# First GLU weights split ahead of the gated rows in halves, one operand's buffers placed lowest, and the last prompt tile's store issued by SP

## The chip, the cores and the metric

One core of a Trainium2 chip runs the whole program; its cores' engines are TensorE (PE, with its weight loads as PEld), VectorE (DVE), ScalarE (ACT), GpSimd (POOL) and SyncE (SP). The metric is the device time of one execution in microseconds, as a median over several runs.

## What is computed

One layer of a hybrid decoder is applied to 512 prompt tokens and to 64 sample tokens (8 sequences of 8), with shared weights. It has an attention branch (three gated branches over compressed, selected and window keys) and a state-space branch; the part of the second that the change touches is the gated linear unit (GLU) behind it, and the merge that follows.

```python
def s5_branch(u, h0_re, h0_im, ssm_par, glu_w, glu_b):
    y, hr, hi = s5_scan(...)
    y = jax.nn.gelu(y.reshape(B, T, D_SSM))
    out = (y @ glu_w[0] + glu_b[0]) * jax.nn.sigmoid(y @ glu_w[1] + glu_b[1])
    return out, hr, hi

def merge_out(x, o_att, z_att, y_ssm, z_ssm, g_merge, w_att_out, w_ssm_out, w_o, ln_g, ln_b):
    p_att = (o_att * jax.nn.silu(z_att)) @ w_att_out
    p_ssm = (y_ssm * jax.nn.silu(z_ssm)) @ w_ssm_out
    g_att, g_ssm = jnp.split(g_merge, 2, axis=-1)
    merged = jax.nn.sigmoid(g_att) * p_att + jax.nn.sigmoid(g_ssm) * p_ssm
    return layer_norm(ALPHA * x + merged @ w_o, ln_g, ln_b)
```

## The kernel before

Every large product is made of three matmuls in a reduced-precision format: each operand is split into a high part, which ACT copies with rounding (L108), and a low part, the difference, which DVE computes (L121, or L124 with a scale). The three matmuls are issued by `mm3` at L129 (high, high), L130 (high, low operand) and L131 (low weights, high). `split` is therefore one ACT instruction and, behind it, one DVE instruction, and the first matmul of a product waits for ACT, the second and third for DVE.

The order of instructions on each engine is not the order of the source. A scheduler with its own timing model places them when the program is built; each engine then works through its list in order, and SP's list is the queue from which most loads are issued.

The work around the change, in order of time:

- The 512 prompt tokens pass attention in four tiles of 128 (`prompt_tile`, i = 0 to 3). Each tile ends by multiplying its accumulator with the gate rows (`ast`, DVE, L1084) and storing the product to the DRAM scratch `aD` (L1085, issued by ACT). `aD` is read again near the end (L1610).
- Then `sample` begins. `attend_setup` loads the selection matrix `selt` (L1217, SP) and multiplies the gates by it (L1220, eight small matmuls on PE). The loads of the state-space rows `y` (L1548, 32 of them) and of the GLU weights `or` (L1511) are held back by `issue_after` until the load of `selt` has been issued.
- The sample attention works on four pairs of sequences (w = 0 to 3). The first three are woven with the compression of cached keys. The last pair is woven with `ssm_out`, which is the GLU and the product with `w_ssm_out`.
- `ssm_out` takes its buffers from a pool that overlies the memory of the compression, which has ended by then: scratch, ring, four pairs of operand buffers `ah`/`al` (`pair(0)` to `pair(3)`), two sets of weight tiles. The order of the first requests sets the order of the addresses.
- It splits the four `y` tiles (128 by 576 elements, written through an access pattern that turns the order of tokens) into `ah`/`al`, one ACT and one DVE instruction each. Then it walks over four column tiles of the GLU weights. `weights` loads 128 by 1024 elements, first half for the linear factor and second half for the sigmoid factor, and splits them in one go. For each half of the tokens (288 each) it makes the sigmoid product first and then the linear one; each product is four `mm3`, so twelve matmuls of 288 columns. One GLU column tile is 48 matmuls.
- `output` forms the attention product, the merge, the product with `w_o` and the layer norm.

Of the kernel before, what the change touches and what calls it, by code (L numbers as in the profile page):

```python
# [85 lines left out]
def rr(ap, pat, **kw):  # L86
    return ap.rearrange(pat, **kw)


class Hybrid:  # L90
# [899 lines left out]
    def prompt_tile(self, i, KT, kczs, vcp, bt):  # L990

        nc, pp = self.nc, self.pp
# [4 lines left out]
        q0 = i * 128  # L997
        n = q0 + 128
# [3 lines left out]
        for br in range(2):  # L1002
            P4s = []
            for g in range(2):
# [3 lines left out]
                for r in range(4):  # L1008
                    p = self.psum("S", [128, 512])
# [37 lines left out]
        p = self.psum("S", [128, 4, 2, 64])  # L1047
# [34 lines left out]
        st = pp.tile([128, 4, 128], F, name="ast", tag="ast", bufs=1)  # L1082
        nc.sync.dma_start(st[:], rr(self.zD[0:4], "r p t -> p r t")[:, :, q0:q0 + 128])
        V.tensor_tensor(st[:], rr(acc[:], "p (r q) -> p r q", r=4), st[:], op=OP.mult)  # L1084
        nc.scalar.dma_start(self.aD[:, :, q0:q0 + 128], st[:])  # L1085


    def gather(self, out, cache, idx):
# [413 lines left out]
        return [p.tile([128, 8, 128], d, name=nm, tag=nm, bufs=2)  # L1502
                for p, nm, d in ((self.py, "or", F), (self.pd, "oh", FR), (self.pd, "ol", FR))]

    def weights(self, pieces):

        w, hi, lo = self.weight_tiles()
        at = 0
        for src, n in pieces:
            with self.tc.issue_after(self.selt_dma.ins):  # L1510
                self.wdma = self.nc.sync.dma_start(w[:, at:at + n, :] if n > 1 else w[:, at, :], src)  # L1511
            at += n
        self.split(hi[:, :at], lo[:, :at], w[:, :at])
        return hi, lo

    def ring(self, d=FR):
# [9 lines left out]
    def ssm_out(self):  # L1526

        nc, A, pd = self.nc, self.A, self.pd
        V, G = nc.vector, nc.gpsimd
        TT, TS, ST = V.tensor_tensor, V.tensor_scalar, V.scalar_tensor_tensor  # L1530
        self.halves = [slice(h * 288, h * 288 + 288) for h in range(2)]

        self.scratch("z")
        self.ring()
        for ct in range(4):
            self.pair(ct)
        self.weight_tiles()
        bg = pd.tile([128, 2, 4], F, name="bg")
        with nc.allow_non_contiguous_dma("bias"):
            nc.sync.dma_start(bg[:], rr(A["ssm_glu_b"], "k (t p) -> p k t", p=128))  # L1540
        TS(bg[:, 1], bg[:, 1], 0.5, None, op0=OP.mult)
        gh, gl = [], []
        for ct in range(4):
            y = self.py.tile([128, TOK], F, name="y", tag="y", bufs=4)
            ys = rr(self.yD[ct * 8:ct * 8 + 8], "g (t c) n -> g c t n", t=8)
            for g in range(8):
                with self.tc.issue_after(self.selt_dma.ins):
                    nc.sync.dma_start(rr(y[g * 16:(g + 1) * 16], "c (t n) -> c t n", t=8), ys[g])  # L1548
            hi, lo = self.pair(ct)
            self.split(rr(hi, "p (n t) -> p t n", t=8), rr(lo, "p (n t) -> p t n", t=8), rr(y[:], "p (t n) -> p t n", t=8))  # L1550
            gh.append(hi)
            gl.append(lo)

        sh, sl = [], []
        gw = rr(A["ssm_glu_w"], "k (t p) c -> p k t c", p=128)
        for ct in range(4):
            c = slice(ct * 128, (ct + 1) * 128)
            hi, lo = self.weights([(gw[:, 0, :, c], 4), (gw[:, 1, :, c], 4)])
            z, th, ln = self.scratch("z"), self.scratch("th"), self.scratch("ln")
            nc.sync.dma_start(z[:], self.zD[4 + ct])  # L1560
            for s in self.halves:
                for k in (1, 0):
                    p = self.bank()
                    for t in range(4):
                        self.mm3(p[:, :288], (hi[:, 4 * k + t], lo[:, 4 * k + t]), (gh[t][:, s], gl[t][:, s]), t == 0, t == 3)
                    if k:
                        self.act(th[:, s], p[:, :288], AF.Tanh, scale=0.25, bias=bg[:, 1, ct:ct + 1])
                    else:
                        self.act(ln[:, s], p[:, :288], AF.Identity, scale=0.5, bias=bg[:, 0, ct:ct + 1])
                    yield  # L1570
            ST(ln[:], th[:], 1.0, ln[:], op0=OP.add, op1=OP.mult)
            G.tensor_tensor(ln[:], ln[:], z[:], op=OP.mult)
            hi, lo, _ = self.ring()
            self.split(hi, lo, ln[:])
            sh.append(hi)
            sl.append(lo)

        ws = rr(A["w_ssm_out"], "(t p) c -> p t c", p=128)
        self.merged = []
        for c2 in range(4):  # L1580
            self.merged += self.ring(F)[0:2]
            hi, lo = self.weights([(ws[:, :, (2 * c2 + u) * 128:(2 * c2 + u + 1) * 128], 4) for u in range(2)])
            for u in range(2):
                ct = 2 * c2 + u
                if ct == 0:
                    self.glu_dma = self.wdma
                tg = self.scratch("tg")
                nc.sync.dma_start(tg[:], self.gD[8 + ct])
                for s in self.halves:
                    p = self.bank()  # L1590
                    for t in range(4):
                        self.mm3(p[:, :288], (hi[:, 4 * u + t], lo[:, 4 * u + t]), (sh[t][:, s], sl[t][:, s]), t == 0, t == 3)
                    ST(self.merged[ct][:, s], tg[:, s], 1.0, p[:, :288], op0=OP.add, op1=OP.mult)
                    yield
# [136 lines left out]
```

## Time and profile before

| what | value |
|---|---|
| median of 3 runs | 892.15 us (891.99 to 892.65) |
| profiled execution | 889.58 us, span from first to last instruction 887.8 us |
| PE busy | 849.6 us (96% of the span), 7276 matmuls |
| DVE busy | 568.8 us (64%) |
| ACT busy | 426.2 us (48%) |
| POOL busy | 196.0 us (22%) |
| mean granted TensorE clock | 0.981 of full |

The profile is taken from one execution by the hardware profiler, and times in it count from the start of its span. A timeline row gives the start, the busy time, the engine, the line, the operation, what it writes and reads and how many instructions were merged; in square brackets stands how long the engine had been idle before it and who released it. In the chain of work a row gives start, length, engine, tile and line of one piece of the chain that ended last. [...]

### The profile page before, as it was taken

Reading aid. Unit: us, or ns where it says so; the run is one execution under the profiler, and the core shown is the slowest. Engines: PE = TensorE matmul, PEld = TensorE weight load, DVE = VectorE, ACT = ScalarE, POOL = GpSimd, SP = SyncE. Lnnn points to the kernel's source line nnn. Section 1 sums busy time; section 2 is a strip of 40 time slices with the busy share of each in tenths; the row PEclk is TensorE's granted clock in tenths of the full one; section 3 lists DMA queues with packets and bytes.
Section 4 is the critical chain, followed back from the end, with each engine's and each line's share of the span. In section 5 each row is a group of like instructions: output and inputs, shape, how many; then the busy total and the mean of one; then the engine's idle time right before and its main releaser. Section 6 shows DMA issues by size and latency. Waiting matters only on the chain.

```text
span 887.8 us, 18479 instructions
## 1 busy us (share of the span) xinstructions
PE 849.6 (96%) x7276; PEld 747.8 (84%) x7276; DVE 568.8 (64%) x1559; ACT 426.2 (48%) x876; POOL 196.0 (22%) x249
## 2 busy tenths in 40 slices
PE   8999999999999988999989999999999979999996
PEld 8999999999999967787757878787878758889885
DVE  3469973855354479988627767766764463448784
ACT  4224462223254365768535656555555565545420
POOL 0322719300042211121211323241321101200000
PEclk9999999999999979999979999999999989999999
DMA  8385526365687352323457746383726164849331
GB/s 279 95 201 165 148 67 193 113 203 150 208 247 239 135 133 96 120 96 120 148 182 216 264 164 261 120 313 116 285 97 238 61 236 145 283 129 277 109 107 48
DMA packets 116039, 151.03 MB, mean 170 GB/s; under 512 B 29352, under 2 KB 93224, under 8 KB 111600
## 3 DMA queue, kind: packets, MB, share of 16 engines
q1 hardware_dynamic: 89072, 65.02, 25.6%
q0 software_dynamic: 17824, 80.16, 25.2%
q10 hardware_dynamic: 9056, 4.67, 1.8%
q8 instruction: 57, 0.93, 0.4%
q14 instruction: 30, 0.25, 0.1%
HBM read 134.02 MB, written 19.93 MB: 173 GB/s over the span
## 4 chain that ended last, share of the span: by engine, by line
PE 65%; DVE 11%; DMA 7%; issue 5%; POOL 4%; ACT 4%; SPq 3%; POOLq 0%; DVEq 0%; ACTq 0%
PE p_mm L130 11%; PE p_mm L129 10%; PE p_mm L131 10%; PE p_tr L135 7%; PE p_S L1237 4%; PE p_ca L129 3%; PE p_ca L131 3%; PE p_ca L130 3%; DVE xt L892 2%; PE p_acc L1246 2%; DMA gc<-in_cache_kv_cmp,idx 2%; PE p_acc L1036 2%; DMA relx<-in_rel_bias 1%; DMA wraw<-in_w_in 1%; DVE evl L121 1%
## 5 line engine op out<-in xcount | busy, mean ns | idle before, releaser
L130 PE MATMUL p_mm<-evl,w1h 128*128 128x256 f32 (+1 forms) x512 | 153.8, 300 | 6.3 <-DVE evl L121 6.2
L129 PE MATMUL p_mm<-evh,w1h 128*128 128x256 f32 (+1 forms) x512 | 151.1, 295 | 1.1 <-ACT w1h L108 0.6
L131 PE MATMUL p_mm<-evh,w1l 128*128 128x256 f32 (+1 forms) x512 | 148.2, 290 | 0.9 <-DVE w1l L121 0.9
L121 DVE TENSOR_TENSOR evl<-xt,evh 128x512 fp32r<-128x512 f32 x128 | 87.0, 684 | 52.1 <-ACT evh L108 51.7
L130 PEld LDWEIGHTS p_mm<-evl,w1h 128*128 128x128 f32 x512 | 98.7, 193 | 24.8 <-DVE evl L121 13.1
L108 ACT ACTIVATE evh<-xt 128x512 fp32r<-128x512 f32 x128 | 80.1, 628 | 79.7 <-PE p_mm L131 75.2
L1091 POOL DMA_INDIRECT gc<-in_cache_kv_cmp,idx x64 | 65.5, 1024 | 206.7 <-DVE xt L892 188.9
L129 PEld LDWEIGHTS p_mm<-evh,w1h 128*128 128x128 f32 x512 | 98.9, 193 | 8.7 <-ACT kt L108 2.4
L131 PEld LDWEIGHTS p_mm<-evh,w1l 128*128 128x128 f32 x512 | 98.6, 193 | 5.8 <-issue 4.1
L892 DVE STREAM_TRANSPOSE xt<-gc 128x256 f32<-128x256 f32 x256 | 90.5, 410 | 5.2 <-DMA gc<-in_cache_kv_cmp,idx 4.6
L131 PE MATMUL p_mm<-xTh,wlo 128*128 128x288 f32 x272 | 81.0, 298 | 0.0
L130 PE MATMUL p_mm<-xTl,whi 128*128 128x288 f32 x272 | 81.0, 298 | 0.0
L129 PE MATMUL p_mm<-xTh,whi 128*128 128x288 f32 x272 | 80.9, 298 | 0.0
L108 ACT ACTIVATE pt<-p_tr 128x512 f32<-128x512 f32 x76 | 43.5, 591 | 29.3 <-PE p_tr L135 29.2
L341 DVE TENSOR_TENSOR wlo<-wraw,whi 128x512 fp32r<-128x512 f32 (+1 forms) x56 | 37.5, 728 | 25.4 <-ACT whi L108 25.4
L1091 POOL DMA_INDIRECT g<-in_cache_kv_slc,idx x32 | 32.6, 1018 | 92.9 <-PE p_acc L1246 65.7
L108 ACT ACTIVATE kt<-p_tr 128x512 f32<-128x512 f32 x72 | 40.7, 594 | 24.2 <-PE p_tr L135 24.2
L130 PEld LDWEIGHTS p_mm<-xTl,whi 128*128 128x128 f32 x272 | 51.3, 189 | 0.2 <-issue 0.2
L129 PEld LDWEIGHTS p_mm<-xTh,whi 128*128 128x128 f32 x272 | 51.3, 189 | 0.2 <-issue 0.2
L108 ACT ACTIVATE whi<-wraw 128x2048 fp32r<-128x2048 f32 (+2 forms) x24 | 37.1, 1563 | 29.9 <-DMA wraw<-in_w_in 9.4
L131 PEld LDWEIGHTS p_mm<-xTh,wlo 128*128 128x128 f32 x272 | 51.4, 189 | 0.0
L135 PE MATMUL p_tr<-cst,P 128*128 128x128 f32 x304 | 47.1, 284 | 0.6 <-ACT P L108 0.5
(527 smaller groups left out, 2105.4 us busy)
## 6 DMA issues: line engine op xcount, KB each, us to landing
wraw<-in_w_in SPq DMA_DIRECT2D x11, 1024.0 KB
wraw<-in_w_in SPq DMA_DIRECT2D x10, 512.0 KB
gD<-zst POOLq DMA_DIRECT2D x16, 288.0 KB, 3.2
tg<-gD SPq DMA_DIRECT2D x16, 288.0 KB
wn<-in_state_win_kv POOLq DMA_DIRECT2D x4, 1024.0 KB, 6.2
wor<-in_w_o SPq DMA_DIRECT2D x8, 512.0 KB
out<-in_state_win_kv SPq DMA_DIRECT2D x8, 504.0 KB
wraw<-in_w_in SPq DMA_DIRECT2D x3, 1056.0 KB
```

The lines of the kernel that those rows point to most:

```text
L108: return self.nc.scalar.activation(out, in_, func, **kw)
L121: eng.tensor_tensor(lo, src, hi.bitcast(F), op=OP.subtract)
L129: mm(out, lhi, rhi, start=start, stop=False, **kw)
L130: mm(out, lhi, rlo, start=False, stop=False, **kw)
L131: mm(out, llo, rhi, start=False, stop=stop, **kw)
L135: return self.nc.tensor.transpose(out, in_, self.ident[:k, :k])
L341: (eng or self.nc.vector).tensor_tensor(lo[:, kl, :n], w[:, kl, :n], hi[:, kl, :n].bitcast(F), op=OP.subtract)
L892: self.nc.vector.transpose(out=out, in_=in_)
L1036: mm = nc.tensor.matmul(acc[gr[g]], self.kvn[:, kt, c0 + g * 64:c0 + (g + 1) * 64], PTs[g][:], start=br == 0 and kt == 0, stop=False, skip ...
L1091: self.nc.gpsimd.indirect_dma_start(out=rr(out, "c s v g d -> c (s v g d)"), out_offset=None, in_=src, in_offset=bass.IndirectOffsetOnAxis ...
L1237: mm = self.nc.tensor.matmul(out[r], self.qb[:, w, r], keys[b], start=True, stop=True)
L1246: self.nc.tensor.matmul(acc[r], PT[:, r], vals(b)[:, g * 64:(g + 1) * 64], start=start, stop=stop, skip_group_check=True)
```

## The change

The store of the last prompt tile (i = 3) is issued by SP; the other three stay with ACT. In `ssm_out` the buffers of the fourth operand pair are requested first and so lie lowest, which moves the other requests up by one pair. The first GLU weights are split before the `y` rows, their second half (sigmoid factor) before their first. The `y` rows are split in halves of 288 tokens, all four operands' first halves ahead of all second halves. The other three GLU weight tiles are split as before. No arithmetic is added or removed.

```diff
@@ prompt_tile
-        nc.scalar.dma_start(self.aD[:, :, q0:q0 + 128], st[:])
+        (nc.sync if i == 3 else nc.scalar).dma_start(self.aD[:, :, q0:q0 + 128], st[:])
@@ weights
-    def weights(self, pieces):
+    def weights(self, pieces, order=(slice(0, 8),)):
...
-        self.split(hi[:, :at], lo[:, :at], w[:, :at])
+        for s in order:
+            self.split(hi[:, s], lo[:, s], w[:, s])
@@ ssm_out
+        self.pair(3)
         self.scratch("z")
         self.ring()
-        for ct in range(4):
+        for ct in range(3):
             self.pair(ct)
...
-            self.split(rr(hi, "p (n t) -> p t n", t=8), rr(lo, "p (n t) -> p t n", t=8), rr(y[:], "p (t n) -> p t n", t=8))
+            ys4.append([rr(v, pat, t=8) for v, pat in ((hi, "p (n t) -> p t n"), (lo, "p (n t) -> p t n"), (y[:], "p (t n) -> p t n"))])
...
+        glu0 = glu_weights(0, order=(slice(4, 8), slice(0, 4)))
+        for n in (slice(0, 36), slice(36, 72)):
+            for ct in range(4):
+                self.split(*[v[:, :, n] for v in ys4[ct]])
...
-            hi, lo = self.weights([(gw[:, 0, :, c], 4), (gw[:, 1, :, c], 4)])
+            hi, lo = glu_weights(ct) if ct else glu0
```

On SP, at the end of the prompt attention (`ast` is the last tile's gated product, `selt` the selection matrix):

```order
 L1083 DMA ast<-zD 128x4x128 x2
+L1085 DMA aD<-ast 512x1x128
 L1217 DMA selt<-cst 64x512
-L1548 DMA y<-yD 16x8x72 x32
+L1555 DMA y<-yD 16x8x72 x32
 L1511 DMA or<-in_ssm_glu_w 128x4x128 x4
```

The store now stands ahead of the load of `selt`, and with it ahead of the 32 `y` loads; from ACT's list, where it stood ahead of the copies `kc` and `kn`, it is gone.

On ACT, where the last pair's window attention hands over to the GLU (`ah` are the operands' high parts, `oh` the weights'):

```order
 L108 ACTIVATE Pn,smw<-Pn,nmw 128x64
-L108 ACTIVATE ah_8725<-y 128x8x72
-L108 ACTIVATE ah_8738<-y 128x8x72
-L108 ACTIVATE ah_8751<-y 128x8x72
-L108 ACTIVATE ah_8764<-y 128x8x72
-L108 ACTIVATE oh<-or 128x1024 x2
+L108 ACTIVATE oh<-or 128x512 x2
+L108 ACTIVATE ah_8725<-y 128x8x36
+L108 ACTIVATE ah_8736<-y 128x8x36
+L108 ACTIVATE ah_8747<-y 128x8x36
+L108 ACTIVATE ah_8758<-y 128x8x36
```

The first operand that a matmul can use is now ready after three instructions instead of five. The second halves follow, then the second weight tile.

On PE, the first GLU products in the changed kernel:

```order
L135 MATMUL p_tr<-cst,Pn 64x128
L129 MATMUL p_mm<-ah_8725,oh 128x288 x2
L130 MATMUL p_mm<-al_8726,oh 128x288
L131 MATMUL p_mm<-ah_8725,ol 128x288
L129 MATMUL p_mm<-ah_8736,oh 128x288
L130 MATMUL p_mm<-al_8726,oh 128x288
L131 MATMUL p_mm<-ah_8725,ol 128x288
L129 MATMUL p_mm<-ah_8736,oh 128x288
```

Two products of the first token half advance together, operand by operand. 34 GLU matmuls and the product `p_S<-pcs` now stand ahead of the window's `p_acc` matmuls; before, it was 27 GLU matmuls, with `p_S<-pcs` behind `p_acc`.

## Rows read from the trace of the kernel before

**Rows 1.** By stretch: us, then busy and (instructions) of PE, PEld, DVE, ACT, POOL.

```profile
455.70:465.80 10.10, 9.72 (x39) 7.76 (x39) 2.73 (x10) 2.42 (x4) 2.13 (x3) 0.50 0.99 354
466.00:705.00 239.00, 233.89 (x2479) 194.69 (x2482) 159.33 (x495) 134.63 (x269) 60.52 (x59) 1.00 0.55 194
717.20:721.90 4.70, 0.04 (x2) 0.02 (x1) 4.12 (x6) 4.70 (x6) 0.00 (x0) 0.63 0.24 101
721.90:725.20 3.30, 3.28 (x12) 2.93 (x13) 3.26 (x5) 2.00 (x5) 0.00 (x0) 0.50 0.10 28
728.90:832.00 103.10, 102.82 (x977) 92.20 (x976) 62.65 (x153) 55.66 (x104) 9.76 (x9) 1.00 0.67 207
```

**Rows 2.** Timeline of PE around the start of the GLU.

```profile
716.95 0.27 PE L135 MATMUL p_tr<-cst,Pn 128*64 128x128 f32 x1
721.88 0.61 PE L129 MATMUL p_mm<-ah,oh 128*128 128x288 f32 x1 [4.66 <-ACT oh L108]
```

**Rows 3.** Timeline of ACT, same place.

```profile
716.65 4.33 ACT L108 ACTIVATE ah<-y 128x576 fp32r<-128x576 f32 x4
720.78 2.00 ACT L108 ACTIVATE oh<-or 128x1024 fp32r<-128x1024 f32 x2
722.68 0.49 ACT L108 ACTIVATE pcs<-pcs,mxc 128x255 f32<-128x255 f32 x1
```

**Rows 4.** Timeline of DVE, same place.

```profile
717.16 0.16 DVE L1451 TENSOR_TENSOR sw<-sw,gr 128x1 f32<-128x1 f32 x1
717.90 3.43 DVE L121 TENSOR_TENSOR al<-y,ah 128x576 fp32r<-128x576 f32 x3 [0.58 <-ACT ah L108]
...
722.44 2.35 DVE L121 TENSOR_TENSOR ol<-or,oh 128x1024 fp32r<-128x1024 f32 x2
724.71 0.16 DVE L1370 RECIPROCAL smc<-smc 128x1 f32<-128x1 f32 x1
```

**Rows 5.** Timeline of ACT: the same kind of copy, 64 elements wide.

```profile
804.89 0.69 ACT L108 ACTIVATE ah<-zs 128x64 fp32r<-128x64 f32 x4 [0.38 <-DVE zs L1606]
805.49 1.05 ACT L108 ACTIVATE woh<-wor 128x1024 fp32r<-128x1024 f32 x1
```

**Rows 6.** Chain of work: GLU matmuls at either clock, and what follows them.

```profile
722.73 0.24 PE p_mm L129
...
726.64 0.13 PE p_mm L130
...
727.43 0.83 PE p_acc L1246 x40
728.26 0.63 PE p_S L1374 x2
```

**Rows 7.** Timeline of PE at the end of the prompt attention.

```profile
452.10 1.07 PE L1078 MATMUL p_acc<-pcT,vcp 32*64 32x512 f32 x4 [0.47 <-ACT pcT L108]
455.03 0.66 PE L1173 MATMUL p_ca<-w,hs 128*128 128x64 f32 x4 [1.86 <-ACT kc L108]
455.62 1.90 PE L1220 MATMUL p_S<-gs,selt 64*128 64x24 f32 x8
```

**Rows 8.** Timeline of ACT, same place.

```profile
453.94 0.52 ACTq L1085 DMA_DIRECT2D aD<-ast  x1
454.50 0.47 ACT L108 ACTIVATE kc<-p_ca,kb 128x255 f32<-128x255 f32 x1 [2.46 <-DVE ml L1401]
```

**Rows 9.** Timeline of SP's DMA issues, 430 to 485 us.

```profile
437.12 0.51 SPq L1217 DMA_DIRECT2D selt<-cst  x1
450.86 30.27 SPq L1548 DMA_DIRECT2D y<-yD  x32
```

**Rows 10.** DMA packets from 454.9 to 456.4 us: queue, packets, MB, share (q10 is ACT's).

```profile
q10 hardware_dynamic: 528, 0.26, 64.3%
q0 software_dynamic: 10, 0.08, 36.2%
```

**Rows 11.** DMA packets from 438.5 to 442.5 us (q1 is SP's).

```profile
q0 software_dynamic: 77, 0.50, 31.3%
q1 hardware_dynamic: 80, 0.13, 15.1%
```

**Rows 12.** Chain of work: matmuls of the compression before and after 466 us.

```profile
465.68 0.21 PE p_mm L131
...
467.35 0.12 PE p_mm L131
```

More of the change, by code (lines that the diff above doesn't have):

```diff
@@ L1541, in ssm_out, with glu_weights @@
         TS(bg[:, 1], bg[:, 1], 0.5, None, op0=OP.mult)
-        gh, gl = [], []
+        gw = rr(A["ssm_glu_w"], "k (t p) c -> p k t c", p=128)
+        def glu_weights(ct, **kw):
+            c = slice(ct * 128, (ct + 1) * 128)
+            return self.weights([(gw[:, 0, :, c], 4), (gw[:, 1, :, c], 4)], **kw)
+        gh, gl, ys4 = [], [], []
         for ct in range(4):
@@ L1549, in ssm_out @@
             hi, lo = self.pair(ct)
-            self.split(rr(hi, "p (n t) -> p t n", t=8), rr(lo, "p (n t) -> p t n", t=8), rr(y[:], "p (t n) -> p t n", t=8))
+            ys4.append([rr(v, pat, t=8) for v, pat in ((hi, "p (n t) -> p t n"), (lo, "p (n t) -> p t n"), (y[:], "p (t n) -> p t n"))])
             gh.append(hi)
             gl.append(lo)
+        glu0 = glu_weights(0, order=(slice(4, 8), slice(0, 4)))
+        for n in (slice(0, 36), slice(36, 72)):
+            for ct in range(4):
+                self.split(*[v[:, :, n] for v in ys4[ct]])
         sh, sl = [], []
-        gw = rr(A["ssm_glu_w"], "k (t p) c -> p k t c", p=128)
         for ct in range(4):
-            c = slice(ct * 128, (ct + 1) * 128)
-            hi, lo = self.weights([(gw[:, 0, :, c], 4), (gw[:, 1, :, c], 4)])
+            hi, lo = glu_weights(ct) if ct else glu0
             z, th, ln = self.scratch("z"), self.scratch("th"), self.scratch("ln")
```

## The prediction

> **What bounds the kernel now.** I read the rows by stretch first. PE is the bound: from 466 to 705 us it is busy 233.89 of 239 us, from 728.9 to 832 us 102.82 of 103.10 [rows 1]. Time is therefore won or lost where PE stands still or runs at half clock, and what PE loses or gains there moves everything behind it. Two such places are touched. From 717.2 to 721.9 PE does nothing, while ACT is busy all of the 4.70 us [rows 1]: the timelines show the last transpose of the window branch at 716.95, then 4.66 us of idle time ended by ACT's `oh` [rows 2], because ACT first makes four `ah` and only then `oh` [rows 3]. After the pause the clock is at 0.50 until about 725.2 [rows 1]. The second place is the end of the prompt attention: PE is idle for 1.86 us before L1173, for `kc` [rows 7], and ACT was held up 2.46 us ahead of `kc` because the store of `aD` stood in front of it, waiting for DVE's `ast` [rows 8]. From 455.7 to 465.8 the clock is again at 0.50 [rows 1].
>
> **Part one, the start of the GLU.** First the prices. On ACT four `ah` of 576 elements take (720.78 - 716.65) / 4 = 1.03 us each, `oh` of 1024 takes (722.68 - 720.78) / 2 = 0.95 [rows 3], and a copy of 64 takes (805.49 - 804.89) / 4 = 0.15 [rows 5]. From 64 and 1024 the cost per instruction is 0.10 us, the rest goes with the elements. So half an `oh` is 0.53 us and half an `ah` 0.57. On DVE `al` is (3.43 us for three) about 1.11 each and `ol` (724.71 - 722.44) / 2 = 1.13 [rows 4]; with the same 0.10 a half is about 0.61.
>
> [...]
>
> New schedule, starting where ACT is free, 716.65 [rows 3]: `oh` halves ready at about 717.2 and 717.8, the first half `ah` at 718.4 to 718.5, the next three 0.57 apart, two of the second halves by 721.2, then `pcs` (0.5 us), the other two by 722.8. DVE is free at 717.3 [rows 4]: `ol` halves to 718.7, first half `al` ready at 719.3, then one per 0.61 with the small operations between, the last second half at 723.9, `pcs` at 724.1. So PE starts at 718.5 instead of 721.88, does two matmuls, and has steady work from 719.35.
>
> How far it gets depends on the clock. A GLU matmul takes 0.24 us at half and 0.13 at full clock [rows 6]. I compare at the end of the window's `p_acc`, when the changed order has done 34 GLU matmuls, `p_S<-pcs` (0.63) and `p_acc` (0.83). The kernel before has done 27 of them, `p_acc` and `p_S` at 728.89 [rows 6]; with the other seven, 7 x 0.13 = 0.9, it would be at 729.8. Three cases:
>
> - The clock falls as before and returns after as much steady work as before, 3.3 us from 721.88 to 725.2, so at 722.65: 2 + 3.3 / 0.24 = 15.75 matmuls by then, 18.25 x 0.13 = 2.4 to 725.0, and 1.46 to 726.5. Gain **3.3 us**.
> - It stays low until 725.2 as in the trace: 2 + 24.5 matmuls by then, 7.5 x 0.13 = 1.0, 1.46, end 727.7. Gain 2.1 us.
> - It never falls, the pause now being 1.3 us and not 4.66: PE then waits for DVE, `pcs` at 724.1, end 725.75. Gain 4.0 us.
>
> I take 3.3; the ends are 2.1 and 4.0.
>
> **Part two, the store on SP.** ACT no longer waits: `kc` can start at 452.1, L1173 right after the `p_acc` that ends at 453.2, and the idle 1.86 us is gone. But the next work on PE, L1220, needs `selt`. Before, SP issued that load at 437.12 [rows 9], long ahead. Now it stands behind the store, which cannot be issued before `ast` is ready, at 453.94 [rows 8]. With one issue of about 0.51 us [rows 9] `selt` is issued at 454.45. Its landing has no row at this place. From below: the store's packets, 0.26 MB issued at 453.94, are through at 456.4 [rows 8, 10], 2.5 us after the issue; `selt` by that lands at 456.95, and L1220 starts 1.3 us later than at 455.62 [rows 7]. From above: `selt` itself, issued at 437.12 beside a POOL gather, had its 0.13 MB moved between 438.5 and 442.5 [rows 9, 11], up to 5.4 us; that gives 459.85, 4.2 us late. I take 1.4, near the lower end, since until 456.4 the gathers have only 10 packets in flight [rows 10]: the DMA engines are nearly free, and `selt` follows the store on SP's queue.
>
> What of the 1.4 us reaches the end: this stretch runs at half clock [rows 1]. If the clock returns at the same moment, the work put off is done at 0.12 instead of 0.21 us per matmul [rows 12], and 1.4 x 0.12 / 0.21 = **0.8 us** is lost; if the return moves along, 1.4. Ends: 0.7 (1.3 late, clock as before) and 4.2. Queued behind the store on SP are also the `y` and `or` loads: they start some 4 us later, took 30.27 us [rows 9], and are not used before 716.65, so they cost nothing.
>
> [...]
>
> **The rest.** The buffers of the fourth operand change no instruction and no duration; they change what the first splits wait for, and in the trace those start the moment ACT is free [rows 3], so I cost this at nothing. The cover is the window's exponentials; without it the price would be the wait of `ah` for its memory, at most the 4.7 us of the pause. Behind 728.9 the scheduler has put attention and GLU matmuls in another order, with the same instructions; PE had 0.28 us of idle time in 103.10 there [rows 1]. I cost it at nothing and give it 0.8 us either way, since PE arrives earlier and the loads for the output stage may not.
>
> **Sum.** -3.3 + 0.8 = -2.5 us. The profiled execution took 889.58 us (span 887.8), which gives 887.1; the median of the runs is 892.15, 2.57 us more than the profiled one, and the forecast stands against that: **889.65 us**. A measurement of this kernel can tell about 0.2%, 1.8 us, from no change.
>
> **The rivals.**
>
> 1. The gain is real but small: the clock stays low until 725.2 (2.1 us) and the return near 465.8 moves with the stall (1.4 us). Sum -0.7: **891.45 us**, no change that can be told. For it: both low stretches follow a pause and lasted 3.3 and 10 us of work [rows 1], and the new start of the GLU has gaps between operands. Against it: 0.5 us and less per gap. Chance 0.31, with neighbouring mixtures.
> 2. Slower: `selt` lands behind the gathers. POOL's transfers start about when the store is through [rows 10]; if `selt` shares the engines with them, it takes what it took before, L1220 is 4.2 us late, and if the clock's return is put off by 3.3 us more than that, (1 - 0.12 / 0.21) of it [rows 12], 1.4, is lost too. With the lower gain of the GLU, 2.1: +3.5, **895.65 us**; it decides against the forecast once the delay on PE at 455.62 passes the gain by 1.8 us. For it: rows 11. Against it: rows 10. Chance 0.11.
> 3. The store costs only its issue: `selt` is there in time, by whatever order the queue takes, and PE keeps 0.52 us of ACT's issue [rows 8]. Then -3.3 - 0.5: **888.35 us**. [...] Rows 7 to 9 leave little room for it. Chance 0.07, on the side of faster.
> 4. The change does not do what it says: a split waits for a load or for memory, and PE starts at 721.9 after all. Then only part two is left, +0.8, **892.95 us**. The `y` and `or` loads are done over 200 us earlier [rows 9]; this is within the 0.31.
>
> **How the numbers follow.** The forecast with its own ends (gain 2.1 to 4.0, loss 0.7 to 1.4, 0.8 for the rest) runs from 888.05 to 892.25 and has 0.51; the two cases of a stronger gain bring faster to 0.58. No change has 0.31, slower 0.11. The range 887.8 to 893.0 takes in the forecast, rivals 1, 3 and 4 and leaves out most of rival 2.
>
> **What would show it.** In the profile of the changed kernel: `aD` on SP's queue near 454 and `selt` half a microsecond behind; `kc` on ACT near 452.1; PE waiting before L1220 until about 457; first GLU matmul some 1.3 us after the last window transpose, not 4.66; `p_acc<-wn` and `p_S<-pcs` together about 2.5 us earlier than at 727.43, counted from 887.8. The prediction is wrong if the first GLU matmul still waits over 3 us, if L1220 starts before 456 or after 458.5, or if PE has more than 1 us of new idle time between 729 and 832.

## The result, and the profile after

The changed kernel takes **899.18 us** (median of 5 runs, 896.46 to 904.72) against 892.15 us before: the ratio is 1.0082, with a 95% interval of 1.0058 to 1.0106. It is slower by 7.0 us, where 2.5 us faster was forecast; the time lies outside the range. Run once more later (e10) it was 898.61 us against 891.98, 1.0064 (1.0036 to 1.0092). The profiled execution took 898.94 us with a span of 897.1 us, 9.3 us more than that of before.

Where the 9.3 us are is found by cutting both spans at the same instructions of PE's timeline. The cuts are the first `p_acc<-pcT` of L1078 in the last prompt tile, the first matmul of L1237 (the product with `kc`), the last window transpose and the first GLU matmul; each figure is a difference of two start times.

```
stretch                                before   changed   difference
start to L1078                         452.10    456.24    +4.14
L1078 to L1237                           5.35     11.33    +5.98
L1237 to the last window transpose     259.50    258.17    -1.33
transpose to the first GLU matmul        4.93      1.50    -3.43
first GLU matmul to the end            165.92    169.86    +3.94
```

**The end of the prompt attention.** PE's timeline of the changed kernel, to be held against [rows 7] (start, us, engine, line, operation, count, and in brackets the idle time with what ended it):

```profile
456.24 1.07 PE L1078 MATMUL p_acc<-pcT,vcp 32*64 32x512 f32 x4 [0.47 <-ACT pcT L108]
457.25 0.66 PE L1173 MATMUL p_ca<-w,hs 128*128 128x64 f32 x4
465.74 1.90 PE L1220 MATMUL p_S<-gs,selt 64*128 64x24 f32 x8 [7.83 <-DMA selt<-cst]
```

L1173 now follows L1078 without a pause: the 1.86 us of [rows 7] are gone, as forecast. L1220 then waits 7.83 us for `selt`. SP's and POOL's timelines say what surrounds that load:

```profile
458.08 0.62 SPq L1085 DMA_DIRECT2D aD<-ast  x1
458.79 0.59 SPq L1217 DMA_DIRECT2D selt<-cst  x1
459.48 6.54 SPq L1555 DMA_DIRECT2D y<-yD  x8
```

```profile
458.09 0.93 POOL L1091 DMA_INDIRECT g<-in_cache_kv_slc,idx  x1 [19.20 <-PE p_ca L1173]
459.33 0.94 POOL L1091 DMA_INDIRECT g<-in_cache_kv_slc,idx  x1 [0.30 <-issue]
460.57 0.94 POOL L1091 DMA_INDIRECT g<-in_cache_kv_slc,idx  x1 [0.30 <-issue]
461.51 0.77 POOL L1331 DMA_DIRECT2D wn<-in_state_win_kv  x1
```

`selt` is issued 0.71 us behind the store (0.51 was forecast), but L1220 starts only 6.95 us after that issue. POOL issues three gathers and a load of 1 MB in the same four microseconds. The DMA view shows the packets of the two queues (q1 is SP's, q0 POOL's), first from 459 to 461 us, then from 461 to 462.6, then from 462.6 to 465.7:

```profile
q1 hardware_dynamic: 528, 0.26, 52.0%
q0 software_dynamic: 12, 0.10, 27.6%
...
q0 software_dynamic: 54, 0.44, 81.9%
q1 hardware_dynamic: 3, 0.01, 1.6%
...
q0 software_dynamic: 118, 0.85, 86.8%
q1 hardware_dynamic: 146, 0.14, 18.4%
```

The 528 packets are the store's. For the next 1.6 us SP's queue moves three packets, `selt`'s first, while POOL's queue holds 81.9% of the DMA engines' time; the rest of `selt` comes through in the third stretch, between POOL's packets. Read packet by packet, its 64 packets of 2 KB run from 462.27 to 464.52 us, 3.5 to 5.7 us after the issue, and L1220 starts 1.2 us behind the last.

**The start of the GLU.** PE's timeline, where [rows 2] had a pause of 4.66 us:

```profile
725.74 0.27 PE L135 MATMUL p_tr<-cst,Pn 128*64 128x128 f32 x1
727.24 0.58 PE L129 MATMUL p_mm<-ah,oh 128*128 128x288 f32 x2 [1.22 <-ACT ah L108]
728.04 0.61 PE L130 MATMUL p_mm<-al,oh 128*128 128x288 f32 x1 [0.23 <-DVE al L121]
```

ACT's and DVE's timelines at that place answer to [rows 3, 4]; a half `ah` is 3.40 / 6 = 0.57 us and a half `ol` 1.29 / 2 = 0.65:

```profile
725.43 1.13 ACT L108 ACTIVATE oh<-or 128x512 fp32r<-128x512 f32 x2
726.47 3.40 ACT L108 ACTIVATE ah<-y 128x288 fp32r<-128x288 f32 x6
```

```profile
726.08 1.29 DVE L121 TENSOR_TENSOR ol<-or,oh 128x512 fp32r<-128x512 f32 x2
727.29 1.92 DVE L121 TENSOR_TENSOR al<-y,ah 128x288 fp32r<-128x288 f32 x3
```

**The clock and the tail.** Three stretches by window (us, then busy time and number of instructions of PE, PEld, DVE, ACT, POOL, granted clock of PE as a share of full speed, busy share of the DMA engines, GB/s), the first two to be read against [rows 1]:

```profile
457.90:475.00 17.10, 8.88 (x37) 7.13 (x37) 2.57 (x15) 2.42 (x4) 3.58 (x4) 0.50 0.91 286
727.60:731.00 3.40, 3.17 (x14) 2.96 (x13) 3.40 (x7) 3.40 (x9) 0.00 (x0) 0.50 0.55 161
810.00:830.00 20.00, 17.45 (x130) 16.96 (x129) 16.40 (x35) 11.64 (x21) 0.00 (x0) 1.00 0.90 266
```

The clock is at half for 17.1 us around the stall instead of 10.1, and for 3.4 us at the GLU instead of some 6.8 (all of 721.9 to 725.2, and the part of the pause that makes its mean 0.63). In the last stretch PE is idle for 2.55 us, where before it was busy nearly all through [rows 1]. PE's waits from the last window transpose to the end:

```profile
PE p_mm L131 <- DVE ol L121: 1.7, 1, 1.7
PE p_mm L129 <- ACT ah L108: 1.2, 1, 1.2
PE p_tr L135 <- DMA g<-in_cache_kv_slc,idx: 0.9, 1, 0.9
PE p_ca L129 <- ACT ah L108: 0.8, 1, 0.8
PE p_mm L130 <- DVE al L121: 0.2, 1, 0.2
```

The 1.2 and 0.2 belong to the start of the GLU. The 1.7 for `ol` and the 0.8 for `ah` lie at 825.69 and 813.63 us, in the output stage, which no instruction of the change touches; the 0.9 is a gather of the last sample attention.

### The profile page after: what moved, and what is told of

Same layout as the page of the kernel before. It is cut to its first block, busy times and chain, and to the rows that moved or that the text cites. A ratio compares the mean times of both kernels' runs of the same rounds, so it can differ in the third digit from the quotient of the medians.

```text
span 897.1 us, 18480 instructions
## 1 busy us (share of the span) xinstructions
PE 849.5 (95%) x7276; PEld 747.4 (83%) x7276; DVE 570.8 (64%) x1564; ACT 426.4 (48%) x881; POOL 194.5 (22%) x249
## 4 chain that ended last, share of the span: by engine, by line
PE 68%; DVE 11%; DMA 8%; issue 4%; POOL 4%; ACT 3%; SPq 1%; DVEq 0%; ACTq 0%; POOLq 0%
PE p_mm L130 11%; PE p_mm L131 10%; PE p_mm L129 10%; PE p_tr L135 8%; PE p_S L1237 4%; PE p_ca L129 3%; PE p_ca L131 3%; PE p_ca L130 2%; PE p_acc L1246 2%; PE p_acc L1036 2%; DMA g<-in_cache_kv_slc,idx 2%; DMA bt<-vD 1%; DMA wraw<-in_w_in 1%; PE p_mm L365 1%; DMA wor<-in_w_o 1%
```

## The experiments

Three causes were open: `selt` (theory A), the tail (B, later T) and the start (C). e1 to e4 and e9 to e11 ran on one chip (number 13 on record), e5 to e8 on a second (4), e12 on a third (9), each time with the kernel before beside them. The chip of the first measurement is not on record. The stretches of each run are those of one profiled execution; two executions of the changed kernel (the first and e10) differ by 1.1 us from the last transpose to the end.

**e1: the GLU part without the store.**

```
-        (nc.sync if i == 3 else nc.scalar).dma_start(self.aD[:, :, q0:q0 + 128], st[:])
+        nc.scalar.dma_start(self.aD[:, :, q0:q0 + 128], st[:])
```

> The changed kernel with the last tile's store back on ACT, the GLU part and the buffers kept. Theory A (the loss is selt, issued behind the store on SP and landing 7 us after its issue): PE waits under 2 us before the selt matmuls, for kc as before, the GLU part gains its 3.3 us, and the run is 2 to 4 us faster than the kernel before. Theory B (the tail: a new order of attention, GLU and output matmuls behind 729 us costs 3 us or more by itself): the wait for selt is gone, but the run is within 1 us of the kernel before, and the profile shows PE idle before ah or ol between 800 and 830 us. Theory C (the start: the first 436 us of the changed kernel are 4 us longer for a reason that belongs to the change): the run is 1 to 2 us slower than before.

Measured: 892.30 us, ratio 1.0002 (0.9979 to 1.0025). PE's timeline has no wait for `selt`, the old wait for `kc`, and the new start of the GLU:

```profile
456.47 1.12 PE L1173 MATMUL p_ca<-w,hs 128*128 128x64 f32 x4 [1.87 <-ACT kc L108]
...
719.44 0.53 PE L129 MATMUL p_mm<-ah,oh 128*128 128x288 f32 x2 [1.22 <-ACT ah L108]
```

The first GLU matmul comes 1.50 us after the last transpose (717.95), so the 3.4 us are there. But from that transpose to the end of the span it takes 171.65 us, where before took 170.85. Theory B's time came true, not A's: the GLU part gains, and the tail takes it all back. The sign that B named did not come: PE does not wait for `ah` or `ol` between 800 and 830 us; its waits behind the start of the GLU are for `ring` (0.9), `tg` (1.0) and the gather (0.7). From the first GLU matmul to the end e1 takes 4.3 us more than before; what is not in these waits was not traced.

**e2: the store on SP alone**, the same line put into the kernel before.

> The kernel before with the last tile's store on SP and nothing else. Theory A: selt is issued about half a us behind the store and lands about 7 us later, PE stands still 6 to 9 us before the selt matmuls and gets back 2 us at kc; 4 to 6 us slower than before. Forecast's own term (selt lands 2.5 to 3 us after its issue): 0.7 to 1.4 us slower. Theory B: within 1 us of before until 729 us.

Measured: 901.57 us, ratio 1.0100 (1.0078 to 1.0122), 9.2 us slower; more than any theory gave. PE's timeline:

```profile
456.88 0.66 PE L1173 MATMUL p_ca<-w,hs 128*128 128x64 f32 x4
464.97 1.90 PE L1220 MATMUL p_S<-gs,selt 64*128 64x24 f32 x8 [7.43 <-DMA selt<-cst]
```

`selt` was issued at 458.42, 6.55 us before L1220, and L1078 to L1237 takes 10.93 us instead of 5.35, +5.6. What A lacked is the other end: from the last window transpose to the end it is 173.48 us, +2.6, with nothing changed in the GLU or behind it. The scheduler has put PE's matmuls behind the GLU start in another order, in answer to one DMA whose place lies 270 us ahead of them, and PE now waits 1.5 us there for `tg`, for which it did not wait before.

**e3: the gathers behind `selt`.**

```
-        self.nc.gpsimd.indirect_dma_start(
+        return self.nc.gpsimd.indirect_dma_start(
...
-            self.gather(out[-1][:], "cache_kv_slc", self.idx2[:, h, t, 2 * w + b:2 * w + b + 1])
+            g = self.gather(out[-1][:], "cache_kv_slc", self.idx2[:, h, t, 2 * w + b:2 * w + b + 1])
+            if w + t + h == 0:
+                self.after(g, self.selt_dma)
```

> The changed kernel, with the first of POOL's three gathers at 458 us made to wait until selt has landed. Theory A1 (selt is slow because the gathers' packets share the DMA engines with it): selt lands 2.5 to 3 us after its issue, PE's wait before the selt matmuls falls from 7.8 us to about 3.5, and the run is 3 to 5 us faster than the changed kernel unless the gathers are then missed later. Theory A2 (selt is slow by its place behind the store on SP, whatever POOL does): selt still lands 6 to 7 us after its issue and the run is as slow as the changed kernel or slower.

Measured: 894.61 us, ratio 1.0027 (1.0007 to 1.0046), 4.6 us less than the changed kernel's 899.18. SP's, then PE's timeline:

```profile
456.15 0.59 SPq L1217 DMA_DIRECT2D selt<-cst  x1
```

```profile
459.08 1.90 PE L1220 MATMUL p_S<-gs,selt 64*128 64x24 f32 x8 [3.81 <-DMA selt<-cst]
```

The store still stands 0.70 us ahead of `selt`, yet L1220 starts 2.93 us after the issue instead of 6.95. From 456.4 to 458.3 us the DMA view has SP's queue alone:

```profile
q1 hardware_dynamic: 666, 0.41, 80.4%
```

PE's order is the changed kernel's, but for 34 of 7276 matmuls. So A1 holds: of the 6.95 us, 4.0 are the gathers' (with the 1 MB load behind them, which is held back too) and 2.9 the load's own, beside the store's packets. The place behind the store is the reason why the load meets the gathers at all.

**e4: `selt` out of the way.** The load, its matmuls and the gate selection move from the set-up of the sample attention to a place ahead of the last prompt tile, with `selt` in a free buffer (`xt`) of the prompt pool; the `y` and `or` loads are queued behind the store.

```
             for i in range(EARLY, 4):
+                if i == 3:
+                    self.gates()
                 tile(i)
...
-            with self.tc.issue_after(self.selt_dma.ins):
+            with self.tc.issue_after(self.store.ins):
```

> The changed kernel, with selt loaded and its four matmuls and the gate selection done ahead of the last prompt tile (in buffers of the prompt pool that are free by then); the y loads are queued behind the store. Theory A: no wait of PE between 452 and 466 us over 1 us, the 2 us of kc kept, the GLU's 3.3 us kept: 3 to 6 us faster than before, unless the tail takes some of it back. Theory B: 0 to 3 us faster than before, with idle PE before ah or ol between 795 and 830 us. Theory C: 1 to 2 us less than the larger figure of A.

Measured: 889.36 us, ratio **0.9964** (0.9950 to 0.9979), 3.0 us faster than before. PE's timeline:

```profile
457.81 0.66 PE L1175 MATMUL p_ca<-w,hs 128*128 128x64 f32 x4
458.72 0.65 PE L1242 MATMUL p_S<-kc,qb 128*64 128x256 f32 x2 [0.25 <-DVE kc L1169]
```

No wait is left but 0.25 us. The eight `selt` matmuls now run at 388.8 us in 0.27 us each, against 0.38 at L1220 in the changed kernel, where the clock is at 0.50. From 744 us on PE has the order of the kernel before, and behind the start of the GLU it waits only for `pcs` (0.4 us at 725) and the gather (1.5 us at 767), which it reaches earlier than before: 169.55 us from the transpose to the end, 1.3 less than before. That is the lower edge of A.

**e5 to e8** ran on a chip on which the kernel before takes 908.91 us, with 272 to 283 us between L1237 and the last window transpose instead of 258 to 260, and idle time on PE that ends with nothing the profile shows (4.7 to 8.6 us before `p_acc` of L1246 alone, which is L1251 in e5 to e7). They are compared with each other and by their ratios, and their stretches of PE one by one; the kernel of e4 itself did not run there.

e5 splits the weights and the rows whole, e6 puts the fourth operand's buffers back; both start from e4.

```
-        glu0 = glu_weights(0, order=(slice(4, 8), slice(0, 4)))
-        for n in (slice(0, 36), slice(36, 72)):
+        glu0 = glu_weights(0)
+        for n in (slice(0, 72),):
```

> The kernel of e4 (selt early, store on SP, GLU weights ahead), with the weights and the rows split whole instead of in halves. Theory D (the 3.8 us come mostly from putting the weights ahead): the first GLU matmul still starts about 1.5 us after the last window transpose, then PE waits about 1 us for the first whole al and is held by DVE afterwards; 0.5 to 1.5 us slower than e4. Rival (halves only cost, eight more instructions of 0.10 us fixed part on ACT and as many on DVE): equal to e4 or 0.5 us faster. The order behind the GLU start also moves, and by e1 and e4 that alone can be worth 2 to 2.5 us behind 730 us; so the stretch to the end of the window's p_acc is what tells the two apart, not the total.

```
-        self.pair(3)
         self.scratch("z")
         self.ring()
-        for ct in range(3):
+        for ct in range(4):
             self.pair(ct)
```

> The kernel of e4 with the fourth operand's buffers back in their old place; ACT's order is the same, PE's differs at a few places behind the GLU. Forecast's own term: 0, the splits start where ACT is free, total as e4 within 0.3%. Rival: the fourth operand's splits wait for the memory of a tile that the window branch still holds, and the idle time before a GLU matmul grows by 1 to 4.7 us.

Measured: e5 909.74 us, ratio 1.0019 (0.9999 to 1.0040); e6 906.02 us, 0.9963 (0.9940 to 0.9985). e6 has e4's ratio, PE's order of e4 matmul by matmul, and its start of the GLU, 1.50 us after the transpose: the buffers are worth nothing that can be told, as forecast. In e5 the first GLU matmul comes after 1.94 us, and PE waits 1.7 us for `ah` and 0.6 for `al` there, in e6 1.2 and 0.3. The halves are thus worth 0.8 us by these waits, and 1.0 us by the start of PE's 81st matmul behind the transpose (9.83 us after it in e6, 10.86 in e5), as theory D has it; putting the weights ahead does the rest of the 3.4. The remaining loss of e5 is again behind that (173.16 us from the transpose to the end, 170.17 in e6), as its expectation allowed.

e7 is e4 with the store back on ACT; e8 is the changed kernel with that store on POOL.

```
-        self.store = (nc.sync if i == 3 else nc.scalar).dma_start(self.aD[:, :, q0:q0 + 128], st[:])
+        self.store = nc.scalar.dma_start(self.aD[:, :, q0:q0 + 128], st[:])
```

> The kernel of e4 with the last tile's store back on ACT. What is left of the store's move once selt is out of its way: by theory A the wait of ACT for ast returns (2.46 us before) and PE waits about 2 us for kc, so 1.2 to 2 us slower than e4 up to 466 us. Rival: the gathers or the y loads take that back, and it equals e4. The order behind 730 us differs from that of e4; if it is worth 2 us either way the total shows that and not the store.

```
-        (nc.sync if i == 3 else nc.scalar).dma_start(self.aD[:, :, q0:q0 + 128], st[:])
+        (nc.gpsimd if i == 3 else nc.scalar).dma_start(self.aD[:, :, q0:q0 + 128], st[:])
```

> The changed kernel with the last tile's store on POOL's queue, ahead of the gathers; selt stays where the kernel before has it on SP. Theory A: ACT is free, selt is there early, and PE stands still under 1 us before the selt matmuls: 1.5 to 2 us less than the GLU part alone up to 466 us (1.4 to 2.5 us for kc gained), and 5 to 8 us faster than the changed kernel, less what the tail's order takes. Rival: the gathers, one us later, are missed by the first sample attention, and PE waits there.

Measured: e7 913.61 us, ratio 1.0047 (1.0029 to 1.0065); e8 912.39 us, 1.0031 (1.0009 to 1.0052). In e7 L1078 to L1242 takes 4.03 us, in e4 and e6 1.92. With `selt` out of the way the store on SP is therefore worth 2.1 us at this place, the idle time before L1173 in [rows 7] and a little more. The totals of e7 and e6 differ by 7.6 us and do not measure it: e7's profile reaches L1078 3.6 us later, and with another order of PE it takes 3.3 us more from the last transpose to the end. In e8 L1078 to L1237 takes 2.59 us, 2.8 less than in the first profile of before and the shortest with `selt` in its old place. But the sample attention behind it takes 283.1 us, against 271.7 to 277.8 in e5 to e7. Whether the gathers, which now stand behind the store on POOL, cause that stays open, since the stretch varies by 6 us among the other three.

**e9 to e11: the tail, on one chip.** e9 is the changed kernel with the GLU's first step woven in one step earlier. Its PE order differs from the changed kernel's only behind the start of the GLU, and from 757 us on (1048 matmuls) it is that of the kernel before. e10 is the changed kernel, e11 is e4.

```
-                self.weave(self.attend(3, store), steps, 32, 4)
+                self.weave(self.attend(3, store), steps, 32, 3)
```

> The changed kernel with its first GLU step written one step of the last attention earlier. The store and selt stay as in the changed kernel; from the first matmul of the SSM output weights on, PE's order is again that of the kernel before. Theory T (the order that the scheduler gives the tail costs the changed kernel 2.5 us of idle time on PE, 0.84 before ah and 1.71 before ol): both waits are gone, no wait over 0.8 us behind 800 us, and the run is 1.5 to 3 us faster than the changed kernel, still 4 to 6 us slower than the kernel before for selt. Rival (the tail's waits come from work that arrives at another time, whatever the order): waits of 2 us or more stay, and the time equals the changed kernel's within 1 us.

> The changed kernel once more, on the chip of e9 and e11. Theory C (its first 436 us are 4 us longer because of the change): the last matmul before the end of the prompt attention is again 3 us or more later than in the other two runs. Rival (that was the one execution): within 2 us of the others, and the total is 7 us slower than before by the selt wait (5.5 to 6 us), the tail (2.5 us) and the GLU's gain (3.3 us).

> The kernel of e4 once more, beside the changed kernel on one chip: 9 to 11 us faster than e10, and 0.3 to 0.4% faster than the kernel before.

Measured: e9 895.20 us, ratio 1.0031 (1.0007 to 1.0055); e10 898.61, 1.0064 (1.0036 to 1.0092); e11 889.66, 0.9970 (0.9952 to 0.9989). In e9 two stretches of the tail, the ones in which the changed kernel waits for `ah` and `ol`, have no idle time:

```profile
804.00:819.00 15.00, 15.00 (x176) 14.57 (x176) 10.04 (x25) 7.33 (x14) 0.00 (x0) 1.00 0.83 237
819.00:834.00 15.00, 15.00 (x115) 15.00 (x114) 15.00 (x33) 8.12 (x16) 0.00 (x0) 1.00 0.88 264
```

The same two of the changed kernel:

```profile
803.36:818.36 15.00, 14.16 (x196) 13.24 (x195) 6.96 (x18) 5.18 (x12) 0.00 (x0) 1.00 0.62 163
818.36:833.36 15.00, 13.29 (x101) 13.06 (x100) 13.98 (x28) 9.80 (x17) 0.00 (x0) 1.00 0.89 282
```

From the last transpose to the end e9 takes 168.27 us, e10 170.26, the changed kernel 171.36, before 170.85. The order is worth 2.0 to 3.1 us there, and with it the GLU part nets 2.6. By the runs e9 is 3.4 us faster than e10, a little over the 1.5 to 3 expected, and 3.2 us slower than the kernel before, under the 4 to 6 expected; the intervals of the two ratios overlap, so the size rests on the stretches and the waits that are gone. Its L1220 waits as long as ever. Theory T holds. e11 is 8.95 us faster than e10, just under the 9 to 11 expected. For the start: e10 reached L1078 at 457.08, e9 at 456.69, e11 at 459.10, so the changed kernel is not the late one.

**e12: the kernel before once more**, one execution.

> The kernel before once more, for its start: the kernel before and the changed one have the same order of instructions up to 436 us, and the profiled execution of before reached the last vcp matmul of the prompt attention at 452.6 us, that of the changed kernel at 456.7 us. Theory C (the change lengthens the start): again 452 to 453 us. Rival (the start varies from one execution to the next): later, 453.5 to 457 us, while the stretches behind it stay as they were: 4.9 us to the kc product, 259.5 us to the last window transpose, 163 us to the end.

Measured: 911.12 us, span 909.3, on a chip on which the kernel before also took 912.82 beside it. L1078 starts at 458.36 us instead of 452.10. So the start of the kernel before can be as late as the changed one's, though this is another chip. On chip 13, e3 has the whole change and reaches L1078 at 453.61 us, no later than e1 (453.53) with the store on ACT. And of the 4.14 us between the first two profiles, 4.1 are there at PE's 901st matmul (110.80 and 114.91 us), over 300 us ahead of the first instruction whose place differs. Theory C in its full size has no support left. To L1237 it is then 5.81 us, to the first GLU matmul after the transpose 4.93 as in the first profile; the sample attention takes 272.8 us and the stretch from the transpose to the end 172.3, which the expectation had as they were; on that chip most stretches are longer.

## Why the prediction was wrong

**Part one held.** The first GLU matmul waits 1.22 us, not 4.66, in every kernel with the halves, and starts 3.4 us earlier; 3.3 was forecast. At the forecast's point of comparison, with 34 GLU matmuls, `p_S<-pcs` and the window's `p_acc` done, the changed kernel is at 735.13, 9.4 us after the transpose at 725.74. Before was at 728.89 with seven fewer [rows 6], so 728.89 - 716.95 + 0.9 = 12.8 us after its own. The gain is 3.4 us. The prices of the halves were about right (0.57 for `ah`, 0.65 for `ol` against 0.57 and 0.61). Two half `ah` cost 1.13 us, one whole 1.03 [rows 3], so the second instruction adds 0.1 us, which is the cost per instruction taken from the row of 64 elements [rows 5]. The clock behaved in two of the three ways listed: 3.4 us at half in the changed kernel, no half clock in e1 (719.5 to 726.5 at 1.00).

**Part two failed, at the landing of `selt`.** The failing step is "I take 1.4, near the lower end, since until 456.4 the gathers have only 10 packets in flight". The issue was nearly right (2.55 us after L1078, forecast 2.35). The landing was read from [rows 10], and that reading fails twice. The ten packets take 36.2% of the engines there and the store's 64.3%, so the engines were full and not "nearly free". And the rows end as the gathers begin. The same view of the kernel before one microsecond on, from 456.4 to 457.5 us, has the gathers alone:

```profile
q0 software_dynamic: 27, 0.22, 60.6%
```

The packets of `selt` moved 3.5 to 5.7 us after its issue, and by then POOL had issued three gathers and a 1 MB load. L1220 came 5.98 us later against L1078, beyond even the upper end of 4.2, which was taken from a load beside one gather [rows 9, 11]. e3 shows that 2.9 us would have been the landing without the gathers, close to the 2.5 of the forecast's lower end; there L1220 comes 1.95 us later against L1078, where the forecast had 1.4. The factor for the clock, 0.8 for 1.4 us, failed too: it let the clock return at the same moment, but the half clock ended at 475.0 us instead of 465.8. Counted from L1237 it lasted 8.4 us before and 7.4 us now, so its end moved along with nearly all of the stall. The stretch behind is 0.8 to 0.9 us shorter than before's in e1, e2 and e3 too, with and without the stall (1.3 us here), so hardly anything of the stall is seen to come back. Rival 2 had the mechanism and the sign, at 0.11, and a size of 4.2 us for what measured 6.0. That `y` and `or` come later cost nothing, as said: no wait for them appears at the GLU.

Rival 3, by which the store costs only its issue, did not come. The choice of the engine cost 6.0 us at this place, where the load that PE waited for stood behind the store, and gained 2.1 us (e7 against e4) where `selt` was loaded early.

**"The rest" failed too.** "I cost it at nothing and give it 0.8 us either way": the tail's new order costs 2.0 to 3.1 us (e9), and 2.6 us in e2, where no other work behind 466 us changed. The rows of a busy PE [rows 1] showed that the old order had no slack to lose on PE, and the forecast read them as safety. The same instructions, in an order in which PE needs `ah` and `ol` before they are ready, leave PE idle; that could not be priced from the trace of before, and its range had to be wider on the side of slower. The buffers at nothing were right (e6).

Two of the three signs that the prediction named for its own failure came: L1220 later than 458.5 (461.6 even with the start's 4.14 us taken off), and over 1 us of new idle time in the tail. The third, a first GLU matmul that still waits over 3 us, did not.

**The sum.** By the stretches, without the start: +6.0 for `selt`, -1.3 in the sample attention, -3.4 at the GLU, +3.9 behind, together +5.2 us, of which 2.0 to 3.1 are the order. The medians differ by 7.0. The other 1.8 us were not traced. The profiled execution of before was 2.57 us under its median, and its start is earlier than those of all runs on chip 13 (452.1 against 453.5 to 459.1 us). But the difference of the medians also passes that of the stretches from L1078 on by 0.8 to 2.6 us in all six runs on chip 13 with the store on SP, and not in e1, so a small effect of the change on the start is not excluded.

## What to carry to other kernels

A DMA that waits for data is not moved alone: what stands behind it on the new queue is issued later too (`selt` at 458.79 us instead of 437.12), and must be priced by the traffic of the moment in which it will then fly, not of the moment in which it was issued before (6.95 us from issue to use beside the gathers, 2.93 without them, e3). Load what the next stage needs ahead of such a store: with `selt` loaded early this change turned from 7.0 us slower to 2.3 to 3.0 us faster (e11, e4), the best version here. A queue with nothing that PE waits for behind the store is the other way, but the one that was tried, POOL's, gained at the place and lost in the total (e8). Where a scheduler orders the work, compare the whole order after a change: one moved DMA changed it 270 us later (e2), and the tail, in which PE had been busy nearly all the time [rows 1], became 2.6 us longer.

## What was unexpected in the hardware

A load of 128 KB that takes 2.9 us from issue to use beside nothing but its own queue took 6.55 to 6.97 us beside three gathers (four runs). In the 1.6 us from 461 us on, SP's queue moved 3 packets and POOL's 54. Packet by packet the 4.0 us between e3 and the changed kernel fall into three parts: the first packet comes 3.47 us after the issue instead of 1.45 (2.0 us more), the 64 packets take 2.25 us instead of 0.81 (1.4 more), and L1220 follows the last by 1.22 us instead of 0.65 (0.6 more).

The packets are drawn out (the 1.4 us) while POOL's queue holds most of the DMA engines' time: 86.8% from 462.6 to 465.7 us, with 18.4% for SP's. How the engines divide their time between the two queues, and what causes the 2.0 us before the first packet and the 0.6 behind the last, was not tried.

The kernel before took 892 us in the first measurement and on chip 13, and 909 to 913 us on chips 4 and 9, with most of the difference in the sample attention (272.8 us in e12, 259.5 in the first profile); its cause was not pursued.
